# A depthwise convolution in a fused two-layer inference step: the 64 sample columns move from 31 taps on VectorE to a product on GpSimd and a sum on VectorE

## The chip, the core and the metric

The kernel runs on one core of a Trainium2 chip. The time is the device time of one execution in microseconds (us). Five engines work beside each other and are tied together by semaphores: TensorE (PE for its matmuls, PEld for its weight loads), VectorE (DVE), ScalarE (ACT), GpSimd (POOL) and SyncE (SP), which issues most DMAs. Each engine takes its instructions strictly in the order in which the program lists them.

## The reference, cut to what matters

The program is one step of two layers for 528 prompt tokens (16 learned ones and 512 of the prompt) and 64 sample tokens (8 sequences of 8), all in fp32. The change lies in layer 0, in the causal depthwise convolution over 31 tokens of 1024 channels:

```
h = u * sigmoid(g)
hp = concatenate([buf, h], axis=1)          # 30 older rows ahead of each sequence
y = conv(hp, conv_w, depthwise) + conv_b    # y[t] = sum over k of conv_w[k] * hp[t + k]
y = silu(layer_norm(y)) @ pw
```

For the prompt the 30 older rows are zeros; each of the 8 sample sequences brings its own 30 rows from a state. Beside the convolution layer 0 has a second branch, a diagonal state space (S5) with a sequential scan over time, and both meet in gates and an output projection.

## The kernel before

Channels lie on the 128 partitions and the 592 tokens along the free axis. A dense product takes 128 output channels at a time (a stripe), in blocks of four 128-row slices of its input. For precision each fp32 weight block is split in two: ACT copies the block `wraw` to `wh` in a rounded format, and DVE subtracts to get the rest, `wl` (`splits` in `dense_threads`). PE then runs 24 matmuls for a block: `xh` by `wh`, `xl` by `wh` and `xh` by `wl`, for four slices and two column spans of 296. There are two buffers of `wh` and of `wl`, so the pair of the block after next can only be made when a block's matmuls are done.

The convolution is done for eight tiles of 128 channels (`convs`, line 1037). A tile `hh` holds 558 columns for the prompt (30 zeros and 528 tokens) and then 8 groups of 38 columns (30 state rows and 8 tokens) for the samples. `conv_taps` (line 831) issues two DVE instructions for each of the 31 taps: one over the 528 prompt columns and one over the 8 by 8 sample columns. Each takes a shifted view of `hh`, times a per-channel weight, plus the running sum in `taps`, which lies in PSUM. The last tap writes to `cc` in SBUF. A prompt tap follows the sample tap of the same number and the other way about, and each needs the result of the one before the last.

POOL does most of S5. `s5_chain` (line 722) walks 66 steps of the scan, each with three small dependent POOL instructions (`s5c`, `s5c`, `s5xv`), twice in the layer (two halves of the state). After a chain POOL copies states to `s5xpad`, which PE needs for its next S5 products. Between the chains POOL builds tables: the products `s5ca` and `s5cb` and the block-diagonal `s5bd` for PE, and then `s5kt`, for which it waits until PE has made a product of them and ACT has copied it out of PSUM. DVE and ACT put the result through a GELU (`s5q`, `s5y`, line 819). POOL also centres each finished convolution tile (`cc<-cc,lna`) and adds it to the sums of the layer norm (`lnb`, `lnc`).

The order of all this on the five engines is set when the program is built. `Weave` (line 263) keeps a list of threads with priorities (line 1098): weight splits first, the convolution next to last, and PE's products last. It books each instruction at a cost of its own table (`cost`, line 239) and always emits what can start first. While fewer than the wanted number of convolution tiles are done, `jobs` (line 978) puts other projection stripes ahead of the next convolution input, so that PE has work. Everything that follows is then fixed: at run time an engine that is late holds up all that stands behind it.

Of the kernel before, what the change touches and what calls it, by code (L numbers as in the profile page):

```python
# [11 lines left out]
F32 = mybir.dt.float32  # L12
F32R = mybir.dt.float32r
I32 = mybir.dt.int32
AF = mybir.ActivationFunctionType
OP = mybir.AluOpType
AX = mybir.AxisListType
# [3 lines left out]
NT = 592  # L21
K1, K2 = 354, 532
NP = 528
# [195 lines left out]
AP = bass.AP  # L219
# [208 lines left out]
def bc(ap, shape):  # L428
    return ap.to_broadcast(shape)
# [398 lines left out]

def conv_taps(K, P, j, h, c, acc):


    cw = P["convw"][:, 31 * j:31 * j + 31]
    b8 = lambda z: z.rearrange("p (b t) -> p b t", b=8)
    hs = b8(h[:, 558:])
    for k in range(31):
        for sl, cut, src in ((slice(0, NP), lambda z: z, h[:, k:k + NP]), (slice(NP, NT), b8, hs[:, :, k:k + 8])):
            o = cut((c if k == 30 else acc)[:, sl])
            if k == 0:  # L840
                yield K.V.tensor_scalar(o, src, cw[:, 0:1], P["convb"][:, j:j + 1], op0=OP.mult, op1=OP.add)
            else:
                yield K.V.scalar_tensor_tensor(o, src, cw[:, k:k + 1], cut(acc[:, sl]), op0=OP.mult, op1=OP.add)


def layer0(K, O):
    nc, tc, I = K.nc, K.tc, K.I
    T, V, A, G, D = K.T, K.V, K.A, K.G, K.D
    mk = lambda name, bufs=1: tc.tile_pool(name=name, bufs=bufs, reuse_waits="tile")
    with mk("l0") as p0:  # L850
        par = p0.tile([128, I["par0"].shape[1]], F32, name="par0")
        P = {k: par[:, a:b] for k, (a, b) in K.at["p0"].items()}
        M = []
        with banks(K, sps=2), mk("ln0") as pl, mk("cc", 8) as pc, mk("zs") as pz, ExitStack() as mid, \
                tc.manual_schedule(engines=MANUAL):
            cv, p5 = (mid.enter_context(mk(n)) for n in ("cv", "s5"))
            w = Weave(K, dict(sps=2, acc=4))
            taps = K.ss.tile([128, 1024], F32, name="taps", bufs=1)
# [4 lines left out]
            X, XR, UB, YB, Z, H, CA, C, Y, GZ = ([] for _ in range(10))  # L863
# [173 lines left out]
            def convs():  # L1037
                for j in range(8):
                    yield lambda: len(H) > j
                    c = pc.tile([128, NT], F32, name="cc")  # L1040
                    yield from conv_taps(K, P, j, H[j], c, taps)
                    S.taps += 1
                    CA.append(c)

# [38 lines left out]
            def loads_y():  # L1083
                yield lambda: S.open
                for j in range(8):
# [11 lines left out]
            q, loads, splits, products, results = dense_threads(K, w, jobs(), X)  # L1097
            w.run([(-1, splits), (-1, splits_x()), (0, results), (1, s5_applied()), (2, s5_tabled()), (3, norms()), (4, loads_y()),
                   (5, loads_z()), (6, loads_x()), (7, loads), (7, consts()), (8, convs()), (9, products)])
        K.lnb0 = K.cp.tile([128, 16], F32, name="lnb0")  # L1100
        nc.vector.tensor_copy(K.lnb0, P["lnb"])
# [1221 lines left out]
```

## Time and profile before

| | |
|---|---|
| median of 3 runs | 2764.46 us (2763.84 to 2769.56) |
| profiled execution, its own time | 2762.25 us |
| its span in the profile | 2760.5 us |
| PE busy | 2624.8 us, 95% of the span |
| DVE busy | 1692.7 us, 61% |
| ACT busy | 1065.4 us, 39% |
| POOL busy | 963.7 us, 35% |
| convolution's first and last instruction begin | 105.4 and 537.7 us from the start |
| instructions on `taps` and `cc` of the convolution | 248 of 128x528 and 248 of 128x64 |

The busy shares are means over the whole span; the convolution lies in one stretch of 430 us near its start, and the shares there are others. Matmuls are pipelined: a record of PE lasts longer than the distance to the next one, so a busy PE is not yet a PE at its full pace. The granted clock is a share of the full 2.4 GHz; 0.5 is the lower level of 1.2 GHz.

### The profile page before, as it was taken

How to read it: one execution, taken by the hardware profiler on the slowest of the kernel's cores; microseconds unless marked ns; L12 is line 12 of the kernel's file. 1: busy time of each engine (PE TensorE's matmuls, PEld its weight loads, DVE VectorE, ACT ScalarE, POOL GpSimd, SP SyncE). 2: the span in 40 equal slices, each digit the busy share in tenths (PEclk: the TensorE clock that was granted, in tenths of full speed). 3: DMA queues.
4: the chain of work that ended last, by engine and by line, in shares of the span. 5: the costliest groups of instructions: out<-in, count | busy, mean ns of one | idle time of the engine just before them, and what ended most of it. 6: DMA issues, size and time to landing. Idle time of an engine off the chain costs nothing. (4 is left out here: it accounts for less than half of the span.)

```text
span 2760.5 us, 49648 instructions
## 1 busy us (share of the span) xinstructions
PE 2624.8 (95%) x18848; PEld 2530.0 (92%) x18848; DVE 1692.7 (61%) x3282; ACT 1065.4 (39%) x2291; POOL 963.7 (35%) x1776
## 2 busy tenths in 40 slices
PE   8998899899999998999999999999999999999996
PEld 8998899899999998998888998998999989898996
DVE  7679798873443357666767667667563444446337
ACT  4322322252222234544545445455333334334223
POOL 1885677510002223244244253245200212212533
PEclk9999999999999999999999999999999999999998
DMA  6333343444333333212222222222333423425333
GB/s 197 94 98 90 99 103 87 98 129 135 114 101 111 104 117 113 85 61 79 71 67 77 75 77 69 65 78 68 100 105 88 138 91 124 140 86 169 115 110 103
DMA packets 202095, 278.33 MB, mean 101 GB/s; under 512 B 66808, under 2 KB 86008, under 8 KB 201856
## 3 DMA queue, kind: packets, MB, share of 16 engines
q1 hardware_dynamic: 199552, 270.30, 32.6%
q10 hardware_dynamic: 2304, 4.85, 0.5%
q8 instruction: 148, 2.42, 0.4%
q14 instruction: 91, 0.75, 0.1%
HBM read 232.54 MB, written 42.53 MB: 100 GB/s over the span
## 5 line engine op out<-in xcount | busy, mean ns | idle before, releaser
L321 PE MATMUL acc<-xh,wl 128*128 128x296 f32 (+2 forms) x3488 | 801.4, 306 | 38.2 <-DVE wl L321 38.2
L321 PE MATMUL acc<-xh,wh 128*128 128x296 f32 (+1 forms) x3520 | 806.2, 306 | 11.4 <-ACT xh L321 6.3
L321 PE MATMUL acc<-xl,wh 128*128 128x296 f32 (+1 forms) x3520 | 806.5, 305 | 0.0
L321 PEld LDWEIGHTS acc<-xh,wl 128*128 128x128 f32 x3488 | 573.9, 191 | 55.0 <-DVE wl L321 47.3
L321 DVE TENSOR_TENSOR wl<-wraw,wh 128x512 fp32r<-128x512 f32 x492 | 375.5, 763 | 381.3 <-ACT wh L321 359.1
L321 PEld LDWEIGHTS acc<-xh,wh 128*128 128x128 f32 x3520 | 582.3, 191 | 18.3 <-ACT xh L321 6.3
L321 PEld LDWEIGHTS acc<-xl,wh 128*128 128x128 f32 x3520 | 582.0, 191 | 5.7 <-issue 2.3
L321 ACT CAST wh<-wraw 128x512 fp32r<-128x512 f32 (+1 forms) x496 | 306.0, 618 | 713.7 <-PE acc L321 629.3
L321 DVE SCALAR_TENSOR_TENSOR taps<-hh,par,taps 128x528 f32<-128x528 f32 x464 | 245.7, 530 | 13.0
L490 PE MATMUL acc<-xh,wh 128*128 128x296 f32 (+2 forms) x832 | 182.1, 299 | 0.0
L490 PE MATMUL acc<-xh,wl 128*128 128x296 f32 (+1 forms) x832 | 180.8, 298 | 0.7 <-DVE wl L434 0.5
L490 PE MATMUL acc<-xl,wh 128*128 128x296 f32 (+2 forms) x832 | 180.5, 297 | 0.0
L433 ACT CAST wh<-wraw 128x512 fp32r<-128x512 f32 x100 | 62.0, 620 | 209.9 <-PE acc L490 207.2
L490 PEld LDWEIGHTS acc<-xh,wl 128*128 128x128 f32 x832 | 131.5, 188 | 1.5 <-DVE wl L434 1.4
L490 PEld LDWEIGHTS acc<-xh,wh 128*128 128x128 f32 x832 | 132.1, 189 | 0.5 <-ACT wh L433 0.2
L490 PEld LDWEIGHTS acc<-xl,wh 128*128 128x128 f32 x832 | 131.9, 188 | 0.4
L434 DVE TENSOR_TENSOR wl<-wraw,wh 128x512 fp32r<-128x512 f32 x100 | 70.0, 701 | 95.9 <-ACT wh L433 90.3
L321 POOL TENSOR_TENSOR rnt<-rcf,rn 128x75 f32<-128x75 f32 (+14 forms) x240 | 87.1, 363 | 84.0 <-DMA rcf<-rcd 67.7
L1155 POOL TENSOR_TENSOR rr<-rr,lna 128x592 f32<-128x592 f32 (+1 forms) x2 | 3.5, 1736 | 309.9 <-ACT lna L404 309.9
L404 POOL TENSOR_TENSOR lnb<-lnb,rr 128x592 f32<-128x592 f32 (+1 forms) x24 | 42.5, 1770 | 186.1 <-DVE rr L1124 186.1
L321 ACT ACT_TABLE_LOAD x71 | 91.1, 1283 | 16.9 <-DVE rh L321 15.0
L321 POOL TENSOR_TENSOR k<-mc,mch 128x512 fp32r<-128x512 f32 x32 | 42.1, 1315 | 157.3 <-ACT mch L321 133.0
(577 smaller groups left out, 4812.4 us busy)
## 6 DMA issues: line engine op xcount, KB each, us to landing
wraw<-w_e SPq DMA_DIRECT2D x160, 256.0 KB, 3.3
wraw<-w_m SPq DMA_DIRECT2D x160, 256.0 KB, 3.0
wraw<-w_r SPq DMA_DIRECT2D x132, 256.0 KB, 3.0
wraw<-w_eo SPq DMA_DIRECT2D x64, 256.0 KB, 2.9
wraw<-w_oo SPq DMA_DIRECT2D x64, 256.0 KB, 3.0
rcf<-rcd SPq DMA_DIRECT2D x16, 640.0 KB
wraw<-w_glu SPq DMA_DIRECT2D x32, 256.0 KB, 2.6
mc<-mc SPq DMA_DIRECT2D x32, 256.0 KB, 3.1
```

The source lines that it names most:

```text
L321: getattr(eng.e, fn)(out, *a, **kw)
L404: getattr(eng.e, fn)(out, *a, **kw)
L433: K.nc.scalar.copy(H, x)
L434: (e or K.nc.vector).tensor_tensor(L, x, H.bitcast(F32), op=OP.subtract)
L490: K.nc.tensor.matmul(o, w[:, kk], x[:, a:b], start=st, stop=sp)
L1155: G.tensor_tensor(r, r, N.c, op=OP.subtract)
```

## The change

The 31 sample taps of a tile go away. In their place the sample columns are worked out in four pieces of two sequences each. For a piece, POOL multiplies 16 overlapping windows of 31 columns (a view of `hh` in which neighbouring windows share 30 columns) by the 31 weights into a new tile `win` of 496 columns, and five prompt taps later DVE sums each window with a `tensor_reduce` into 16 columns of `cc`. There is one buffer of `win`. At the end of a tile ACT adds the bias to the 64 columns. The prompt taps stay as they were.

```diff
-def conv_taps(K, P, j, h, c, acc):
-    cw = P["convw"][:, 31 * j:31 * j + 31]
-    b8 = lambda z: z.rearrange("p (b t) -> p b t", b=8)
-    hs = b8(h[:, 558:])
+def windows(z):
+    part_, (sb, nb), (st, _) = z.ap
+    return AP(z.tensor, z.offset, [part_, [sb, nb], [st, 8], [st, 31]])
+
+def conv_taps(K, P, pool, j, h, c, acc):
+    V, G = K.V, K.G
+    cw, b = P["convw"][:, 31 * j:31 * j + 31], P["convb"][:, j:j + 1]
+    hs = h[:, 558:].rearrange("p (b t) -> p b t", b=8)
+    sh = [128, 2, 8, 31]
+    acc = acc[:, 0:NP]
     for k in range(31):
-        for sl, cut, src in ((slice(0, NP), lambda z: z, h[:, k:k + NP]), (slice(NP, NT), b8, hs[:, :, k:k + 8])):
-            o = cut((c if k == 30 else acc)[:, sl])
-            if k == 0:
-                yield K.V.tensor_scalar(o, src, cw[:, 0:1], P["convb"][:, j:j + 1], op0=OP.mult, op1=OP.add)
-            else:
-                yield K.V.scalar_tensor_tensor(o, src, cw[:, k:k + 1], cut(acc[:, sl]), op0=OP.mult, op1=OP.add)
+        src = h[:, k:k + NP]
+        if k % 8 == 0:
+            i = k // 4
+            z = pool.tile(sh, F32, name="win", bufs=1)
+            yield G.tensor_tensor(z, windows(hs[:, i:i + 2]), bc(cw[:, None, None, :], sh), op=OP.mult)
+        if k == 0:
+            yield V.tensor_scalar(acc, src, cw[:, 0:1], b, op0=OP.mult, op1=OP.add)
+        else:
+            yield V.scalar_tensor_tensor(c[:, 0:NP] if k == 30 else acc, src, cw[:, k:k + 1], acc, op0=OP.mult, op1=OP.add)
+        if k % 8 == 5:
+            yield V.tensor_reduce(c[:, NP + 8 * i:NP + 8 * i + 16].rearrange("p (b t) -> p b t", b=2), z, axis=AX.X, op=OP.add)
+    yield K.A.activation(c[:, NP:NT], c[:, NP:NT], AF.Identity, bias=b)
...
-                    yield from conv_taps(K, P, j, H[j], c, taps)
+                    yield from conv_taps(K, P, cv, j, H[j], c, taps)
```

The order is planned anew, so it differs on every engine from the first convolution tile to the end of S5. On DVE, the start of the first tile before (`wl` is the rest of a weight block that PE waits for):

```order
L321 TENSOR_SCALAR taps<-hh,par_73 128x528
L321 TENSOR_SCALAR taps<-hh,par_73 128x64
L321 SCALAR_TENSOR_TENSOR taps<-hh,par_73,taps 128x528
L321 SCALAR_TENSOR_TENSOR taps<-hh,par_73,taps 128x64
L321 SCALAR_TENSOR_TENSOR taps<-hh,par_73,taps 128x528
L321 SCALAR_TENSOR_TENSOR taps<-hh,par_73,taps 128x64
L321 SCALAR_TENSOR_TENSOR taps<-hh,par_73,taps 128x528
L321 TENSOR_TENSOR wl<-wraw,wh 128x512
L321 SCALAR_TENSOR_TENSOR taps<-hh,par_73,taps 128x64
L321 SCALAR_TENSOR_TENSOR taps<-hh,par_73,taps 128x528
```

and the same place on DVE now:

```order
L321 TENSOR_SCALAR taps<-hh,par_73 128x528
L321 SCALAR_TENSOR_TENSOR taps<-hh,par_73,taps 128x528 x4
L321 TENSOR_TENSOR wl<-wraw,wh 128x512
L321 SCALAR_TENSOR_TENSOR taps<-hh,par_73,taps 128x528
L321 TENSOR_REDUCE cc<-win 128x16
L321 SCALAR_TENSOR_TENSOR taps<-hh,par_73,taps 128x528
L321 TENSOR_TENSOR wl<-wraw,wh 128x512
L321 SCALAR_TENSOR_TENSOR taps<-hh,par_73,taps 128x528
```

The sample taps are gone, a prompt tap now follows the prompt tap that it needs, and a sum stands ahead of the second `wl`. On POOL, the table stretch after the first chain, around the wait of `s5kt` for PE and ACT, before:

```order
L321 MEMSET hh 128x30
L321 MEMSET s5kt 32x4x112
L321 TENSOR_TENSOR s5dm<-cst,s5par 32x64
L321 TENSOR_TENSOR s5kt<-s5kt,s5dm 32x4x16
L321 TENSOR_TENSOR s5ca<-s5cr,k_515 128x576
```

and the same place on POOL now:

```order
L321 TENSOR_TENSOR lnb<-lnb,cc 128x592
L321 TENSOR_TENSOR lnc<-lnc,st 128x592
L321 TENSOR_TENSOR win<-hh,par_73 128x496
L321 MEMSET s5kt 32x4x112
L321 TENSOR_TENSOR s5dm<-cst,s5par 32x64
L321 TENSOR_TENSOR s5kt<-s5kt,s5dm 32x4x16
L321 TENSOR_TENSOR win<-hh,par_73 128x496
L321 TENSOR_TENSOR s5ca<-s5cr,k_515 128x576
```

A product of the convolution stands on either side of the wait. In the first S5 chain the products stand between its dependent steps, on POOL now:

```order
L321 TENSOR_TENSOR s5c_1719<-s5a_799,s5xv 128x64
L321 TENSOR_TENSOR win<-hh,par_73 128x496
L321 TENSOR_TENSOR s5c_1720<-s5c_1719 128x32
L321 TENSOR_TENSOR s5xv<-s5xv,s5c_1720 128x32
L321 TENSOR_TENSOR s5c_1763<-s5a_799,s5xv 128x64
```

Of the 32 products, 8 stand between the `s5kt` ahead of the first chain and that chain's end, and 7 between the same places of the second. PE's order holds 698 projection matmuls in the first of these stretches where it held 608, and 703 in the second where it held 621; what stands behind them has become less by as much. From the last part of layer 0 on, every engine's order is the same as before.

## Rows read from the trace of the kernel before

**Rows 1.** The page's first part: busy us (share of the span) xinstructions.
```profile
PE 2624.8 (95%) x18848; PEld 2530.0 (92%) x18848; DVE 1692.7 (61%) x3282; ACT 1065.4 (39%) x2291; POOL 963.7 (35%) x1776
```

**Rows 2.** Busy time by stretches: from:to, length, engines' busy us (instructions), PEclk, DMA.
```profile
105.00:540.00 435.00, 393.66 (x2795) 383.41 (x2794) 377.80 (x663) 105.02 (x200) 304.05 (x623) 0.97 0.37 96
540.00:600.00 60.00, 56.80 (x411) 55.64 (x410) 48.58 (x65) 33.30 (x52) 20.42 (x20) 1.00 0.44 123
650.00:700.00 50.00, 50.00 (x368) 50.00 (x367) 17.96 (x31) 13.32 (x23) 0.00 (x0) 1.00 0.41 125
...
126.10:219.40 93.30, 86.49 (x609) 83.35 (x608) 73.67 (x138) 20.13 (x37) 74.81 (x201) 1.00 0.33 93
378.90:472.10 93.20, 87.25 (x618) 84.31 (x617) 82.30 (x155) 20.21 (x38) 77.87 (x201) 1.00 0.34 95
```

**Rows 3.** Waits from 100 to 600 us: who waited for whom, us, times, longest.
```profile
POOL s5kt L321 <- ACT s5kt L321: 42.0, 7, 14.5
POOL cc L321 <- DVE cc L321: 40.0, 5, 18.8
PE acc L321 <- DVE wl L321: 38.2, 34, 5.1
```

**Rows 4.** DVE groups by shape, 105 to 540 us: xcount | busy us, mean ns.
```profile
L321 DVE SCALAR_TENSOR_TENSOR taps<-hh,par,taps 128x528 f32<-128x528 f32 x232 | 179.1, 772 | 7.4
L321 DVE TENSOR_TENSOR wl<-wraw,wh 128x512 fp32r<-128x512 f32 x97 | 83.0, 856 | 30.8 <-ACT wh L321 26.4 <-DMA s5ul<-ub 4.4
L321 DVE SCALAR_TENSOR_TENSOR taps<-hh,par,taps 128x64 f32<-128x64 f32 x232 | 66.6, 287 | 5.7
L321 DVE TENSOR_TENSOR s5q<-s5q,s5y 128x592 f32<-128x592 f32 x6 | 17.2, 2873 | 0.0
L321 DVE TENSOR_SCALAR s5y<-s5y 128x592 f32<-128x592 f32 x6 | 7.1, 1186 | 0.1
```

**Rows 5.** DVE groups by shape, 600 to 850 us, where POOL is nearly idle.
```profile
L321 DVE TENSOR_TENSOR wl<-wraw,wh 128x512 fp32r<-128x512 f32 x70 | 48.3, 690 | 88.0 <-ACT wh L321 87.9
...
L321 DVE TENSOR_TENSOR sz<-sz,sa 128x592 f32<-128x592 f32 x8 | 6.2, 775 | 0.3
...
L321 DVE TENSOR_SCALAR sa<-sa 128x592 f32<-128x592 f32 x8 | 3.8, 470 | 0.9
```

**Rows 6.** DVE timeline, from 168 us: start, length, three pairs of taps merged.
```profile
168.18 3.36 DVE L321 SCALAR_TENSOR_TENSOR taps<-hh,par,taps 128x64 f32<-128x64 f32 x6
```

**Rows 7.** DVE groups by shape over the whole span: the only reduction.
```profile
L321 DVE TENSOR_REDUCE rdg<-rh 128x80 f32<-128x320 f32 x16 | 11.5, 720 | 0.5
```

**Rows 8.** POOL groups by shape, 105 to 540 us: two products of 512 columns.
```profile
L321 POOL TENSOR_TENSOR s5wa<-s5wa,s5t 128x512 f32<-128x512 f32 x4 | 6.1, 1530 | 0.2
...
L321 POOL TENSOR_TENSOR s5wa<-s5rr,k 128x512 f32<-128x512 f32 x4 | 4.2, 1056 | 3.0 <-PE sps L321 3.0
```

**Rows 9.** POOL timeline: ends of the wait before each chain, and copies behind it.
```profile
126.16 0.31 POOL L321 TENSOR_TENSOR s5kt<-s5kt,s5dm 32x64 f32<-32x64 f32 x1 [2.17 <-ACT s5kt L321]
...
215.17 2.16 POOL L321 COPY s5xpad<-s5xv 64x264 f32<-64x264 f32 x8
...
378.92 0.31 POOL L321 TENSOR_TENSOR s5kt<-s5kt,s5dm 32x64 f32<-32x64 f32 x1 [3.35 <-ACT s5kt L321]
...
469.46 2.63 POOL L321 COPY s5xpad<-s5xv 64x264 f32<-64x264 f32 x8
```

**Rows 10.** PE timeline: the first matmuls on what each chain left.
```profile
219.45 0.41 PE L321 MATMUL sps<-s5xpad,s5ca 128*128 128x148 f32 x2
...
472.16 0.41 PE L321 MATMUL sps<-s5xpad,s5ca 128*128 128x148 f32 x2
```

**Rows 11.** DVE timeline, from 255 us: one product of two SBUF tiles.
```profile
255.78 4.68 DVE L321 TENSOR_TENSOR s5q<-s5q,s5y 128x592 f32<-128x592 f32 x1
```

**Rows 12.** PE timeline, from 515 us: a wait, and matmuls behind it.
```profile
515.61 0.86 PE L321 MATMUL acc<-xh,wl 128*128 128x296 f32 x2 [5.02 <-DVE wl L321]
516.27 0.69 PE L321 MATMUL acc<-xh,wh 128*128 128x296 f32 x2
```

## The prediction

> **What bounds the kernel now.** I first read the page's busy shares: PE is at 95% of the span, everything else far below [rows 1]. Time can be won only where PE is not at its pace, so the second view is the table of stretches. The pace itself stands in a stretch without trouble: 368 matmuls in 50 us at full clock, 0.1359 us each [rows 2]. In the stretch of the convolution, 105 to 540 us, PE issues 2795 matmuls; at that pace they need 379.8 us, and the stretch is 435.0 us long, so 55 us are lost. From 540 to 600 us 411 matmuls need 55.9 of 60, another 4. These 59 us are the ceiling of any gain here.
>
> The third view says who holds PE up. 38.2 us of idle PE from 100 to 600 us end with DVE's `wl` [rows 3], in 34 waits of 1.1 us on average. The rest is in part clock: the granted share is 0.97 there [rows 2], about 13 of 435 us. The lower clock follows long waits: behind the wait of 5.02 us the next pair of matmuls comes 0.66 us later [rows 12], where full pace gives 0.27. So PE loses its time because DVE makes `wl` late.
>
> Why DVE is late stands in its groups. It is busy for 377.8 of 435 us [rows 2], and the largest part is the convolution: 232 large taps of 772 ns and as many small ones of 287 ns (with the eight first and eight last taps it is 248 of each) [rows 4]. Three pairs of taps take 3.36 us [rows 6], which is 1.06 us of work a pair and gaps of 0.035 us. The small tap does an eighth of the columns for over a third of the time of a large one. The convolution is low in priority and fills whatever DVE leaves, so there is no idle time in which a late DVE catches up.
>
> POOL matters in two places. Between the wait for `s5kt` and PE's first use of `s5xpad` lies a chain of small steps: 126.16 to 219.45 and 378.92 to 472.16 us. POOL's last copies end at 217.3 and 472.1 us, 2.1 and 0.1 us ahead of PE [rows 9, 10]. POOL has hardly any room there, though the waits blame DVE. Elsewhere it has: 42.0 us of waits for `s5kt`, 40.0 for finished tiles [rows 3].
>
> **The change part by part.** *Small taps.* 248 go, each 0.287 us [rows 4] and a gap of 0.035. A large tap now follows the one that it needs; the pairs show that two instructions pace each other at 0.035 us already, so I book no new wait: 0.322 x 248 = 80 us of DVE time. If a dependent large tap needed a further 0.1 us, 25 us of that would be gone; nothing in rows 6 shows it, so that is the low end.
>
> *Sums.* 32 reductions of 496 columns to 16. The only one in the trace takes 720 ns for 320 columns to 80 results [rows 7]. Scaled by columns that is 1.12 us; a product of 512 columns takes 0.690 us undisturbed [rows 5], scaled 0.67. The sum has fewer results than the known one, so it should be near the lower row: I take 0.75, 24 us in all (21 to 36). DVE is relieved by 56 us (19 to 59).
>
> *Products.* 32 on POOL, 496 columns. With operands that repeat columns 512 take 1.056 us, with two full ones 1.530 [rows 8]: 1.02 to 1.48. Here the windows are full and the weights repeat: 1.25, 40 us in all. Where POOL waits this is hidden (17 of the 32); in the two chains it is not.
>
> *Bias.* Eight additions on ACT, which is busy for 105 of 435 us [rows 2]: nothing, except when ACT stands there waiting for the last sum with weight casts behind it, which belongs to the third rival.
>
> *The chains, on the path.* Before, PE issued 609 and 618 matmuls in 93.3 us and 93.2 us [rows 2]: at full pace 82.8 and 84.0, so it lost 10.5 + 9.2 = 19.7. Now the plan gives it 90 and 82 more there, 95.0 and 95.1 us of work. POOL needs 91.1 + 8 x 1.25 = 101.1 us and 2 until PE starts, so about 102, and 93.2 + 7 x 1.25 = 101.9. POOL is what is late next: PE loses 7 + 7 = 14. The chains give back 6 of their 20 us.
>
> *Outside the chains.* 59 - 20 = 39 us are lost there now. With 56 us less on DVE, about half of them outside the chains, most waits of a microsecond go. What stays is DVE standing beside a busy POOL: `s5q` takes 2.873 us on average and once 4.68 [rows 4, 11], where a like product takes 0.775 with POOL idle [rows 5]; `s5y` takes 1.186 against 0.470. Over eight tiles that is 8 x (2.10 + 0.72) = 22.5 us of DVE time in a few lumps, and the new products make POOL denser. I leave 19 of the 39 lost.
>
> The row shows that `wl` takes 856 ns beside POOL and 690 without it [rows 4, 5], while no tap takes more than its usual time. [...]
>
> *Sum.* 6 + 20 = 26 us off the profiled execution's own 2762.25 us (a span of 2760.5 and 1.75 around it), 2736. The median of the runs is 2.2 above that execution, so I forecast 2738.5 us.
>
> **The rivals.** *Nearly all comes back.* The freed DVE time absorbs the lumps as well, and a product costs 1.02 us. Then POOL needs 91.1 + 8.2 + 2 = 101.3 and 93.2 + 7.1 = 100.3 us in the chains, PE loses 6 + 5, and outside about 5: 59 - 16 = 43 off, 2721.5. For it: the gap of 55 us is about what DVE is freed of. Against it: single waits of 5 us as in rows 12 come from `s5q`, which the change doesn't touch.
>
> *POOL takes it back.* A product costs 1.48 us and 0.5 of being blocked, 2.0; the chains lose 91.1 + 16 + 2 - 95 = 14 and 93.2 + 14 - 95.1 = 12, and outside of them 17 products each hold a `wl` for part of their length, 30 in place of 19. Then 59 - 56 = 3 off, 2761.5, no change. For it: `s5wa` with full operands is at 1.53, and POOL is busy for 304 of 435 us. Against it: the mean of `wl` is only 0.17 above its undisturbed length, although POOL is busy for 70% of that stretch.
>
> *Slower: DVE now waits in POOL's queue.* In the table stretches a product stands behind `s5kt`, which waits for PE and ACT; 42.0 us of such waits in seven, the longest 14.5 [rows 3]. The sum of that product stands five large taps later on DVE (4.0 us), with `wl` behind it. When the wait is longer than that, DVE stands, PE gets no weights, and PE's stand makes the next wait of POOL longer. If 38 of the 42 us come through to PE, the loss is 33 + 38 = 71 against 59: 12 us slower, 2776.5. It decides from 26 us on. For it: the single `win` buffer ties both engines every eight taps. Against it: the planner puts a product early, where POOL idles, and PE is usually ahead of the wait by then.
>
> **How the numbers follow.** The likeliest gets 0.54, with a range of its own of 2728 to 2750. Nearly all comes back: 0.20. POOL takes it back: 0.12. Slower: 0.14. A measurement of this kernel tells about 0.2%, 5.5 us, from no change. Faster by more: 0.54 + 0.20 and 0.02 of the second rival, 0.76; within: 0.10; slower: 0.14. The range goes from 2713, where the ceiling of 59 us is nearly reached, to 2768, which holds the second rival and the near end of the third; most of the third and a little below are left out.
>
> **What would show it.** DVE busy between 105 us and the last tap lower by about 56 us against the same work; large taps still at 0.77 us with 0.035 between them; sums near 0.75, products near 1.25. `PE <- DVE wl` down from 38 to some 15 us, and new waits of PE for POOL of 5 to 8 us at the two first uses of `s5xpad`. Fewer stretches at the lower clock. The first rival is right if those POOL waits are missing; the second if products are near 2 us or `wl` is near 1 us; the third if DVE's waits for `win` add up to over 26 us. I am wrong altogether if PE's loss up to 600 us is not smaller than 59 us, or if time changes behind layer 0, where every order is as before.

## The result, and the profile after

The changed kernel takes 2730.95 us (median of 4 runs, 2726.44 to 2734.66) against 2766.74 of the kernel before beside it (2763.84 to 2769.56): a ratio of 0.987, 95% interval 0.985 to 0.989, 36 us less. 2738.5 was forecast. The profiled execution has a span of 2729.7 us, 30.8 less than before. The sum was nearly right; the reason behind it was not, as the experiments show, so the nearness is in good part luck.

Busy time over the whole span, as in [rows 1]:

```profile
PE 2614.5 (96%) x18848; PEld 2525.8 (93%) x18848; DVE 1647.1 (60%) x3066; ACT 1066.3 (39%) x2297; POOL 1006.1 (37%) x1808
```

The stretches that answer to [rows 2], the two chains last (from the `s5kt` behind the wait to PE's first `s5xpad`):

```profile
105.00:540.00 435.00, 413.78 (x3023) 408.42 (x3022) 349.57 (x470) 119.82 (x228) 349.16 (x657) 0.99 0.39 102
540.00:600.00 60.00, 59.39 (x445) 59.29 (x446) 38.31 (x56) 25.52 (x43) 16.81 (x17) 1.00 0.48 133
...
125.70:225.10 99.40, 96.41 (x700) 95.33 (x698) 80.60 (x115) 23.61 (x45) 85.71 (x212) 1.00 0.36 99
389.70:491.20 101.50, 97.81 (x700) 96.81 (x699) 78.43 (x119) 23.32 (x45) 87.75 (x213) 0.98 0.32 94
```

PE issues 3023 matmuls from 105 to 540 us where it issued 2795. At 0.1359 us each that is 410.8 of 435 us: 24 are lost, not 55. From 540 to 600 us nothing is lost. So 35 of the 59 us are won, and PE's first matmul on the finished convolution shows the same, first of before, then of after:

```profile
670.54 0.44 PE L321 MATMUL acc<-cbh,wh 128*128 128x296 f32 x2
```
```profile
634.86 0.44 PE L321 MATMUL acc<-cbh,wh 128*128 128x296 f32 x2
```

That is 35.7 us. Behind it the orders are the same; 5 us are given back there in this one profile. That is within the scatter: behind the last matmul on the finished convolution the profiles of all kernels here have 1926 to 1938 us left, before 1933 and after 1937.5.

The waits from 100 to 600 us, against [rows 3]:

```profile
DVE wl L321 <- ACT wh L321: 68.1, 39, 6.3
...
POOL s5kt L321 <- ACT s5kt L321: 27.0, 7, 12.9
...
PE acc L321 <- DVE wl L321: 18.9, 11, 4.2
...
DVE taps L321 <- POOL hh L321: 12.2, 2, 6.1
```

PE's waits for `wl` halve (38.2, 34 times, before), GpSimd's for `s5kt` fall from 42.0 to 27.0, and VectorE now stands for 68 us itself, waiting for `wh`. The last line is a wait of the first tap of a tile, taken up by an experiment. VectorE's groups from 105 to 540 us, against [rows 4], and GpSimd's product:

```profile
L321 DVE SCALAR_TENSOR_TENSOR taps<-hh,par,taps 128x528 f32<-128x528 f32 x232 | 178.1, 768 | 4.8
L321 DVE TENSOR_TENSOR wl<-wraw,wh 128x512 fp32r<-128x512 f32 x109 | 104.2, 958 | 59.7 <-ACT wh L321 59.6
L321 DVE TENSOR_REDUCE cc<-win 128x16 f32<-128x496 f32 x32 | 21.1, 660 | 0.0
L321 DVE TENSOR_SCALAR sg<-sg 128x592 f32<-128x592 f32 x7 | 10.4, 1481 | 0.0
...
L321 DVE TENSOR_TENSOR s5q<-s5q,s5y 128x592 f32<-128x592 f32 x6 | 6.7, 1123 | 0.1
```
```profile
L321 POOL TENSOR_TENSOR win<-hh,par 128x496 f32<-128x496 f32 x32 | 39.8, 1242 | 18.1 <-DVE cc L321 6.9 <-DMA s5ul<-ub 5.1 <-DVE hh L321 4.0
```

A sum takes 0.66 us and VectorE never waits for a product (idle 0.0 before the sums). `s5q` is down from 2873 ns, `wl` up from 856 and `sg` from 524, by its line in the kernel before:

```profile
L321 DVE TENSOR_SCALAR sg<-sg 128x592 f32<-128x592 f32 x7 | 3.7, 524 | 0.0
```

The lumps beside GpSimd have moved more than they have shrunk.

**Where the time came from** is seen in one cycle of VectorE. PE needs a new `wl` for each block of 24 matmuls, every 24 x 0.1359 = 3.26 us. In the timeline of before, the cycle from one `wl` to the next is too long by 0.6 us:

```profile
171.44 0.68 DVE L321 TENSOR_TENSOR wl<-wraw,wh 128x512 fp32r<-128x512 f32 x1
172.04 3.36 DVE L321 SCALAR_TENSOR_TENSOR taps<-hh,par,taps 128x64 f32<-128x64 f32 x6
175.31 0.68 DVE L321 TENSOR_TENSOR wl<-wraw,wh 128x512 fp32r<-128x512 f32 x1
```

After, at the same place (this first `wl` is stretched beside GpSimd):

```profile
169.10 1.17 DVE L321 TENSOR_TENSOR wl<-wraw,wh 128x512 fp32r<-128x512 f32 x1
170.19 2.38 DVE L321 SCALAR_TENSOR_TENSOR taps<-hh,par,taps 128x528 f32<-128x528 f32 x3
172.47 0.69 DVE L321 TENSOR_TENSOR wl<-wraw,wh 128x512 fp32r<-128x512 f32 x1
```

Counted in the timeline from 105 to 540 us before, 33 of 97 cycles hold three whole pairs of taps; their median is 3.87 us, and 33 x 0.61 = 20 us of the 59. After, up to the last tap, 42 of 101 hold three prompt taps; their median is 3.16, which fits. The question is why: because VectorE has less to do, or because of how many taps the planner puts between two `wl`.

### The profile page after: what moved, and what is told of

Same layout as the page of the kernel before. It is cut to its first block, busy times and chain, and to the rows that moved or that the text cites. A ratio compares the mean times of both kernels' runs of the same rounds, so it can differ in the third digit from the quotient of the medians.

```text
span 2729.7 us, 49466 instructions
## 1 busy us (share of the span) xinstructions
PE 2614.5 (96%) x18848; PEld 2525.8 (93%) x18848; DVE 1647.1 (60%) x3066; ACT 1066.3 (39%) x2297; POOL 1006.1 (37%) x1808
## 5 line engine op out<-in xcount | busy, mean ns | idle before, releaser
L321 DVE TENSOR_TENSOR wl<-wraw,wh 128x512 fp32r<-128x512 f32 x492 | 390.4, 794 | 383.7 <-ACT wh L321 364.0
L321 DVE SCALAR_TENSOR_TENSOR taps<-hh,par,taps 128x528 f32<-128x528 f32 x232 | 178.1, 768 | 4.8
L434 DVE TENSOR_TENSOR wl<-wraw,wh 128x512 fp32r<-128x512 f32 x100 | 70.0, 701 | 96.6 <-ACT wh L433 91.0
L321 ACT ACT_TABLE_LOAD x69 | 88.5, 1283 | 17.5 <-DVE rh L321 15.7
```

Source lines behind the costliest of these rows:

```text
L321: getattr(eng.e, fn)(out, *a, **kw)
L434: (e or K.nc.vector).tensor_tensor(L, x, H.bitcast(F32), op=OP.subtract)
```

## The experiments

Gains are against the kernel before, run on the same chip in the same session; ratios have 95% intervals.

**No sample part at all.**

```diff
-            z = pool.tile(sh, F32, name="win", bufs=1)
-            yield G.tensor_tensor(z, windows(...), ...)
...
-            yield V.tensor_reduce(c[:, NP + 8 * i:...], z, axis=AX.X, op=OP.add)
-    yield K.A.activation(c[:, NP:NT], c[:, NP:NT], AF.Identity, bias=b)
+    yield K.A.activation(c[:, NP:NT], h[:, NP:NT], AF.Identity, bias=b)
```

> Left out: the whole sample part of the convolution (no products on GpSimd, no sums, the 64 sample columns of cc get other data), so VectorE is freed of the 80 us of small taps and nothing is put in their place. Theory A (TensorE lost time because VectorE was overloaded; the new work costs little): the changed kernel already won 31 to 36 us of 59, and what is left there are lumps of VectorE standing beside GpSimd's S5 tables, which stay; so this kernel gains 33 to 42 us on the kernel before, at most 8 us more than the change. Rival B (GpSimd's products hold TensorE up in the two S5 chains and beside the weight splits): without them 48 us or more come off. Rival C (the gain is a lucky order, not the load): any value, also less than 25 us.

Measured: 2726.32 against 2768.57, ratio 0.985 (0.984 to 0.987), 42 us faster, the upper edge of theory A. PE reaches its first `cbh` at 634.45 us, 0.4 from the changed kernel. Products and sums, 40 and 21 us of work, cost PE nothing that can be seen: rival B falls. That VectorE's load decided is not shown by it; 21 us less load brought nothing more there.

**The old small taps added as a load.**

```diff
+        if k == 0:
+            yield V.tensor_scalar(old, hs[:, :, 0:8], cw[:, 0:1], b, op0=OP.mult, op1=OP.add)
+        else:
+            yield V.scalar_tensor_tensor(old, hs[:, :, k:k + 8], cw[:, k:k + 1], old, op0=OP.mult, op1=OP.add)
```

> The changed kernel with the 248 small taps put back on VectorE as a load whose result nobody reads; products and sums stay. VectorE has then 80 us more than in the changed kernel and 24 more than before. Theory A (the gain is VectorE's time): the gain is gone, 0 to 20 us slower than the kernel before, and TensorE waits for wl 35 us or more between 100 and 600 us. Rival D (the gain comes from the plan, which puts 90 and 82 more projection matmuls ahead of the two first uses of s5xpad, and not from VectorE's load): 20 us or more of the gain stay.

Measured: 2751.11, ratio 0.994 (0.993 to 0.996), 17.5 us faster than before, although VectorE is busy for 29 us more than before over the span (1721.9 against 1692.7). Theory A, which was the prediction's, had 0 to 20 us slower. It fails here. Rival D asked for 20 us or more and just misses; PE's waits for `wl` are 30.8 us, where theory A had 35 or more.

**Products twice, and zeros on VectorE.** Two edits of the changed kernel, each for itself:

```diff
             yield G.tensor_tensor(z, windows(hs[:, i:i + 2]), bc(cw[:, None, None, :], sh), op=OP.mult)
+            yield G.tensor_tensor(z, windows(hs[:, i:i + 2]), bc(cw[:, None, None, :], sh), op=OP.mult)
...
-                    yield G.memset(h[:, 0:30], 0.0)
+                    yield V.memset(h[:, 0:30], 0.0)
```

> The changed kernel with each of the 32 products computed twice on GpSimd, 40 us more there, of which some 18 us lie in the two S5 chains. Theory A (GpSimd's time in the chains is covered, since the plan, which books it, lets TensorE have as much more projection work ahead of s5xpad): at most 8 us slower than the changed kernel, so 24 to 36 us faster than the kernel before; the chains get 9 us longer each, and TensorE has no wait of over 2 us at the first uses of s5xpad. Rival B (GpSimd is what is late in the chains): 15 to 20 us slower than the changed kernel, 12 to 20 us faster than before, with waits of 5 us or more at the first uses of s5xpad.

> The changed kernel with the eight memsets of hh's 30 zero columns on VectorE in place of GpSimd. In the changed kernel VectorE stands for 6.1 us twice (at 200 and at 460 us) because this memset lies behind scan steps in GpSimd's queue, and TensorE loses 2.6 us each time. Theory A: these two waits go, 4 to 6 us faster than the changed kernel, 35 to 42 us faster than before. Rival (the first tap waits there for GpSimd anyway, or the new order brings another stall of the same size): within 2 us of the changed kernel.

Measured: twice, 2737.66, ratio 0.989 (0.988 to 0.991), 31 us faster. In the chains it costs nothing (PE's longest wait for `s5xpad` is 1.2 us, its first `cbh` comes at 631.8). The price comes later, where PE has no projection left and waits for the last tiles:

```profile
PE acc L321 <- ACT cbh L321: 8.5, 3, 3.7
...
PE sps L321 <- POOL s5xpad L321: 1.7, 2, 1.2
```

Zeros on VectorE: 2726.95, ratio 0.986 (0.984 to 0.988), which overlaps with the changed kernel's. The two waits of 6 us go, and PE waits 6.1 us for `s5xpad` in their place (twice, 3.1 at most). Undecided.

**Products on VectorE.**

```diff
-            yield G.tensor_tensor(z, windows(hs[:, i:i + 2]), bc(cw[:, None, None, :], sh), op=OP.mult)
+            yield V.tensor_tensor(z, windows(hs[:, i:i + 2]), bc(cw[:, None, None, :], sh), op=OP.mult)
```

> The changed kernel with the 32 products on VectorE in place of GpSimd. VectorE gets 32 x 0.7 to 0.96 us = 22 to 31 us back, GpSimd loses 40. What the chip showed so far: the changed kernel 31 to 36 us faster than the kernel before, 42 us without any sample part, 17.5 us with the old small taps added (24 us more on VectorE than before). Theory A (VectorE's time sets the gain, and by these points about a third of a microsecond for each that VectorE is given): 20 to 32 us faster than the kernel before, PE's waits for wl 20 to 30 us. Rival E (what wins is the form, few wide instructions in place of many small ones, on whichever engine): within 4 us of the changed kernel, 33 us or more faster. Rival F (GpSimd's taking it over is the whole gain): under 15 us.

Measured: 2748.07, ratio 0.993 (0.991 to 0.994), 19.6 us faster, at the edge of A and between E and F. It tells nothing apart.

**The kernel before, its small taps priced.** Only a number of the planner changes:

```diff
+    if fn == "scalar_tensor_tensor" and n == 64:
+        return 0.32
     return 0.07 + n / (1920 if fast else 960) + 0.06 * cols
```

> The kernel before, with one number of the planner changed: a small tap is booked at 0.32 us, as the trace has it with its gap, in place of 0.20. Same instructions, other order. Theory A (load): VectorE is as busy as before, so at most 8 us faster than the kernel before. Rival C (the plan of before runs ahead of a VectorE that it books too low, and the change wins by taking these instructions out of the plan): 15 us or more faster, which would also say why the run with the old taps added kept 17.5 us.

Measured: 2743.95, ratio 0.991 (0.990 to 0.993), 23.7 us faster with the very instructions of before. Rival C holds, load does not. The next two runs take both halves: the right prices on the old instructions, and a wrong price on the new ones.

```diff
+    if any(z.name.startswith("taps") for z in ins):
+        return 0.81 if n == NP else 0.32
```

> The kernel before, same instructions, with the prompt tap booked at 0.81 us and the sample tap at 0.32, together the 1.13 of the trace. With the sample tap alone priced it was 23.7 us faster. Theory P: 22 to 34 us faster than before. Theory L: at most 8. If that one run was a lucky order: under 15.

```diff
+    low = 0.25 if n == NP and any(z.name.startswith("taps") for z in ins) else 0.0
-    return 0.07 + n / (1920 if fast else 960) + 0.06 * cols
+    return 0.07 + n / (1920 if fast else 960) + 0.06 * cols - low
```

> The changed kernel, same instructions, with one number of the planner changed: a prompt tap is booked 0.25 us too low, 62 us in all, about as much as the planner was wrong by on a pair of taps before (0.88 booked, 1.13 in the trace, 248 pairs). Theory P (TensorE loses time where VectorE runs behind the plan by which the order was made, so a good part of the gain is that the change took badly priced instructions out of the plan): 10 to 24 us of the gain go, so 10 to 24 us faster than the kernel before. Theory L (VectorE's load alone decides): within 6 us of the changed kernel, 30 us or more faster than before.

Measured: the old instructions with right prices 2730.72, ratio 0.988 (0.986 to 0.989), 33 us faster; the new ones with a wrong price 2762.71, ratio 0.999 (0.998 to 1.000), nothing left of 36, which is more than theory P (the planner's prices) had, 10 to 24 us. As gains in us:

| | taps booked too low | taps booked as in the trace |
|---|---|---|
| two taps of before | 0 | 33.3 |
| product and sum | 1.3 | 35.8 |

VectorE's cycle shows why. Old instructions, right prices: two pairs between two `wl`, 2.73 us a cycle, inside PE's 3.26:

```profile
168.69 0.68 DVE L323 TENSOR_TENSOR wl<-wraw,wh 128x512 fp32r<-128x512 f32 x1
169.29 2.22 DVE L323 SCALAR_TENSOR_TENSOR taps<-hh,par,taps 128x64 f32<-128x64 f32 x4
171.42 0.68 DVE L323 TENSOR_TENSOR wl<-wraw,wh 128x512 fp32r<-128x512 f32 x1
```

New instructions, wrong price: four prompt taps, 3.70 us a cycle:

```profile
167.19 0.68 DVE L322 TENSOR_TENSOR wl<-wraw,wh 128x512 fp32r<-128x512 f32 x1
167.79 3.19 DVE L322 SCALAR_TENSOR_TENSOR taps<-hh,par,taps 128x528 f32<-128x528 f32 x4
170.89 0.68 DVE L322 TENSOR_TENSOR wl<-wraw,wh 128x512 fp32r<-128x512 f32 x1
```

The stretch from 105 to 540 us, first the old instructions with right prices, then the new ones booked low:

```profile
105.00:540.00 435.00, 413.38 (x3023) 410.11 (x3021) 377.64 (x652) 114.72 (x217) 303.33 (x631) 0.98 0.40 105
```
```profile
105.00:540.00 435.00, 396.69 (x2803) 383.74 (x2801) 336.55 (x449) 114.46 (x214) 321.78 (x619) 0.98 0.34 93
```

and PE's waits for `wl` from 100 to 600 us, in the same order:

```profile
PE acc L323 <- DVE wl L323: 13.5, 7, 4.6
```
```profile
PE acc L322 <- DVE wl L322: 39.2, 36, 5.3
```

VectorE busy for 377.6 us, as much as before, goes with 3023 matmuls, exactly as many as the changed kernel has; VectorE busy for 336.6, less than the changed kernel's 349.6, goes with 2803 and the old 39 us of waits. With the old instructions and right prices the convolution ends later (its last tap at 565 us, 538 before, 506 after), and PE doesn't notice, since it has projections left.

The count of long cycles follows the gain through the other kernels with pairs of taps, from 105 to 540 us:

| | cycles with three whole pairs | gain, us |
|---|---|---|
| before | 33 of 97 | 0 |
| old taps added | 17 of 104 | 17.5 |
| small taps priced | 7 of 103 | 23.7 |
| both taps priced | 3 of 106 | 33.3 |

With the new instructions booked low, 39 of 100 cycles hold four prompt taps or more; in the changed kernel 14 of 108 do.

**What is left: VectorE beside GpSimd's tables.** In the changed kernel's timeline of VectorE single instructions are stretched to five to seven times their undisturbed length (0.69 us for `wl` in [rows 5], 0.52 for `sg`) while GpSimd makes tables:

```profile
290.44 3.19 DVE L321 TENSOR_TENSOR wl<-wraw,wh 128x512 fp32r<-128x512 f32 x1
293.55 3.23 DVE L321 TENSOR_SCALAR sg<-sg 128x592 f32<-128x592 f32 x1
...
524.20 4.80 DVE L321 TENSOR_TENSOR wl<-wraw,wh 128x512 fp32r<-128x512 f32 x1
```

The third costs PE a wait at once:

```profile
529.05 0.54 PE L321 MATMUL acc<-xh,wl 128*128 128x296 f32 x2 [3.02 <-DVE wl L321]
```

First the products of the tables were left out, then put on VectorE:

```diff
-    yield G.tensor_tensor(ca0, cr, pr, op=OP.mult)
...
+    yield G.memset(ca0, 0.01)
```
```diff
-    yield G.tensor_tensor(ca0, cr, pr, op=OP.mult)
+    yield K.V.tensor_tensor(ca0, cr, pr, op=OP.mult)
...
```

> The changed kernel, with the products of the S5 tables (s5wa, s5wb, s5ca, s5cb and s5t on GpSimd, some 80 us there) left out: the tables are filled by memsets, so S5 gives other numbers. Theory A (what is still lost, 24 us, is mostly VectorE standing beside these products: sg 3.07, s5y 2.18 and wl 3.19 and 4.80 us in single pieces): no wl, sg, s5y or s5q over 1.5 us remains beside the tables, and the kernel is 8 to 18 us faster than the changed one, 42 to 52 us faster than before. Rival G (the lumps are due to something else, and the products only happen to lie there): within 5 us of the changed kernel.

> The changed kernel with the products of the S5 tables on VectorE in place of GpSimd: 72 instructions of some 0.65 us, 47 us more on VectorE; GpSimd is freed of some 90 us outside the chains. If the lumps are due to the two engines beside each other, VectorE gets some 15 us of them back. Theory A: the load of VectorE is then 32 us above the changed kernel and 24 below before; by a third of a microsecond for each, and no lumps, within 8 us of the changed kernel, 28 to 40 us faster than before. Rival H (VectorE's load outweighs the lumps): under 22 us faster than before.

Measured: without them 2713.58, ratio 0.980 (0.979 to 0.982), 54 us faster, a little more than theory A had. From 105 to 540 us nine of `wl`, `sg`, `s5y` and `s5q` still last over 1.5 us, the longest `wl` 2.28, where 20 did: theory A had none left, so only part of the lumps is due to the products, the longest among them. On VectorE 2721.61, ratio 0.983 (0.981 to 0.985), 46 us faster, the best kernel that computes everything, and more than either theory had (28 to 40, under 22). Its groups on VectorE, 105 to 540 us:

```profile
L321 DVE TENSOR_TENSOR wl<-wraw,wh 128x512 fp32r<-128x512 f32 x109 | 86.3, 793 | 47.6 <-ACT wh L321 46.9 <-DMA s5ul<-ub 0.2
...
L321 DVE TENSOR_SCALAR sg<-sg 128x592 f32<-128x592 f32 x7 | 3.6, 520 | 0.0
```

VectorE does more than in the changed kernel (360.7 against 349.6 us) and PE waits 5.6 us for `wl` instead of 18.9.

**Two more orders.** The kernel with the tables on VectorE and `wl` booked at 0.72, and the kernel before with both taps priced and the tables on VectorE:

```diff
+    if out.dtype == F32R and n == 512:
+        return 0.72
```

> The changed kernel with the products of the S5 tables on VectorE (46 us faster than before), and wl booked at 0.72 us in place of 0.60, which is its undisturbed length with a gap. Theory P (a plan nearer to the trace is a better order): 46 to 56 us faster than before. Rival (what is left are waits of another kind, weight casts on ScalarE and the ends of chains, and a new order brings others): within 4 us of 46, or less.

> The kernel before with both taps priced as in the trace and the products of the S5 tables on VectorE: no GpSimd products of the convolution, no sums, and VectorE carries some 45 us more than before and 100 more than the changed kernel, about 410 of 435 us. Theory P with the lumps (VectorE's load matters little as long as the plan knows it and GpSimd doesn't stand in its way): 20 to 40 us faster than before. Theory L (VectorE full): 5 us or more slower than before.

Measured: with `wl` priced 2727.69, ratio 0.987 (0.986 to 0.989), 36 us faster. By gains that is 10 us behind the kernel without this price, by bare times 6 us, and PE's first `cbh` comes 4 us later. Theory P had 46 to 56 us and misses: a truer price is no guarantee, and another order alone moves this kernel by some 4 to 10 us. The second: 2761.29, ratio 0.999 (0.998 to 1.000), neither theory's number. PE's waits up to 700 us say where the gain went:

```profile
PE acc L323 <- ACT cbh L323: 27.5, 8, 10.3
PE acc L323 <- ACT wh L323: 9.0, 2, 6.5
```

No wait of PE's matmuls for `wl` is left, and PE issues its first `cbh` at 640.1, 30 us earlier than before. But the convolution ends only at 613 us, PE has run out of projections, stands for 10.3 us, and works through the first tiles at half the clock as they come:

```profile
600.00:640.00 40.00, 29.84 (x212) 29.11 (x211) 29.56 (x42) 13.88 (x24) 17.36 (x11) 0.93 0.28 92
640.00:680.00 40.00, 21.66 (x70) 16.45 (x70) 31.21 (x41) 20.26 (x25) 0.67 (x1) 0.51 0.37 81
```

So a late end of the convolution has a price once the projections no longer reach that far. That VectorE's load made it late is not shown: up to 615 us VectorE stands for 58.6 us waiting for `wh` here, and another order might have ended the convolution sooner.

## Why the prediction came out right, and where it was wrong

- *The ceiling* held: 59 us, of which 35 were won.
- *Durations* held. The small taps went without a new wait (a prompt tap 768 ns, three in a row 2.38 us). The sums took 0.66 us for 0.75, near the lower row as argued; the products 1.24 us for 1.25. VectorE's busy time fell by 45.6 us over the span (1692.7 to 1647.1); the 56 forecast held 9 us of gaps between taps, which do not count as busy.
- *The chains.* The sum slips by 1 us: 101.1 and 2 make 103.1, not 102. POOL needed 99.4 and 101.5 us for the forecast 102. PE lost 4.3 and 6.4 us (700 x 0.1359 = 95.1), 10.7 in place of 14, and the expected waits of 5 to 8 us for `s5xpad` are not there. So 9 of the 20 us came back, not 6; the loss was sized by letting PE stand until all copies were made, and its first matmul begins at 225.06, while the last copies still run.
- *Outside the chains* 24 - 11 = 13 us are lost, where 19 were left: 26 won for 20. Half-clock time fell too (granted share 0.97 to 0.99).
- **The step that failed is the reason**: "So PE loses its time because DVE makes `wl` late" is true, but "Why DVE is late stands in its groups" is not. Lateness was ascribed to load, and the gain of the outside term to "56 us less on DVE". The table of the four gains above shows that the load was not needed: with the old load and right prices the gain is the same, and with the small load and a wrong price it is gone. The planner had booked a pair of taps at 0.88 us (0.07 + 528/960 + 0.06 and 0.07 + 64/960 + 0.06); the trace had 1.13. So it put three pairs between two `wl` where two fit. The change happened to replace the mispriced pair by an instruction whose booked start-to-start distance (0.68 and the 0.13 that the planner lets pass between two dependent ones) is the measured 0.81.
- Two rows that stood ahead of the prediction spoke against it. In [rows 6] three pairs take 3.36 us, and with a `wl` that is 4.0 by lengths, against a block of 3.26; it was read as the price of a pair only. In [rows 4] VectorE stands for 26.4 us waiting for ScalarE's `wh`, and the sentence "there is no idle time in which a late DVE catches up" passes over it: where an engine is late and idle in the same stretch, its order is to be doubted before its load.
- *Luck.* By the prediction's reason, the old load with right prices gains nothing and the new load with a wrong price gains all; they gained 33.3 and 1.3 us. The forecast came within 8 us of this change because the mispriced pair went with the small taps.
- *The rivals.* The third asked for over 26 us of waits for `win`; there were none. The second asked for products of 2 us; it fell too, though `wl` came near its mark (958 ns) and the lumps of 3 to 5 us stand beside POOL's tables, where it had looked to the new products. The first had the POOL waits missing, as it asked, but its 2721.5 is further off than the forecast. None named the planner's prices.
- Open: why the plan with the old taps added, at the same wrong price, puts only half as many triple pairs between two `wl`, which goes with the 17.5 us that it kept; and how much of any one figure is the luck of an order. One change of order was worth 4 to 10 us, so that table's two small differences (1.3 and 2.5) say only that the form of the work is worth little here.

## What to carry to other kernels

Before crediting an engine's load, set one cycle against the other: the time between two deliveries against what the consumer takes for one; an engine that is late in its cycle and idle elsewhere is a case for another order first. Where the order is planned from a table of prices, run the kernel before with the prices of its own trace first, since every change of instructions also changes what the planner believes. A truer price can still give a worse order, as `wl` did here, so the time decides. And look at the end of the stretch too: a convolution that ends late costs nothing until PE's stock of other work is used up.

## What the runs showed of the hardware

A VectorE instruction beside GpSimd's table products can be held up over several of them. During the `wl` of 4.80 us, from 524.20 to 529.00, GpSimd ran on without a gap, products and copies in turn:

```profile
524.31 1.41 POOL L321 TENSOR_TENSOR s5ca<-s5ca,s5t 128x576 f32<-128x576 f32 x1
525.67 0.39 POOL L321 COPY s5xpad<-s5xv 64x264 f32<-64x264 f32 x1
526.03 1.15 POOL L321 TENSOR_TENSOR s5cb<-s5cr,s5npi 128x576 f32<-128x576 f32 x1
527.13 0.20 POOL L321 COPY s5xpad<-s5xv 64x32 f32<-64x32 f32 x1
527.30 1.15 POOL L321 TENSOR_TENSOR s5t<-s5ci,k 128x576 f32<-128x576 f32 x1
```

The prompt taps, with one operand in PSUM, kept means of 767 to 773 ns and the sums of 660 to 663 in every kernel, while `sg`, an in-place multiply and add with a single SBUF input, has a mean of 1481 ns in the changed kernel and of 520 with the tables on VectorE. The Trainium skill (SBUF — State Buffer, Who interferes with whom) counts `tensor_scalar` among the operations that can take the port shared with GpSimd, and `tensor_reduce` not; the traces agree with both. The prediction had counted lumps for `s5q` and `s5y`, and none for `sg`.
